# Two output projections as seven products of half blocks, with sums of weight blocks formed in DRAM

## The chip, the cores and the metric

The kernel runs on one core of a Trainium2 chip. The metric is device time in microseconds (us) of one execution, and the median of several runs is quoted. The engines are TensorE (PE, matmuls; its weight loads are listed as PEld), VectorE (DVE), ScalarE (ACT), GpSimd (POOL) and SyncE (SP, which here only issues transfers). Work is handed from engine to engine by semaphores, and each engine runs its own list of instructions in order.

## What is computed

A trunk of two layers on 512 tokens of 1024 channels, in float32. Each layer is: RMS norm, one wide input projection, mixers with gates, one output projection from 2048 to 1024 channels, residual add. A last RMS norm follows. What matters here are the two output projections:

```python
def even_layer(x, norm_g, w_in, pool_w, pool_scale, ws, bs, w_out):
    h = rmsnorm(x, norm_g)
    z = h @ w_in
    ...
    return x + jnp.concatenate([y_a, y_b], axis=-1) @ w_out

def odd_layer(x, norm_g, w_in, conv_w, w_out):
    ...
    return x + jnp.concatenate([y_c, y_d], axis=-1) @ w_out

def reference(...):
    ...
    return rmsnorm(h, final_norm)
```

## The kernel before, in words

Tokens are cut into four tiles of 128, channels into tiles of 128. Every operand of a large product is split into a high part (rounded to the type float32r, a copy on ScalarE) and a low part (the rest, a subtraction on VectorE); a product is the sum of three matmuls: high by high, high by low, low by high (`mm3`, lines 87 to 90). Weights come in chunks of 1 MB (128 partitions x 2048 elements): `weights` (line 68) loads a chunk on SP's queue into one of three `raw` buffers (line 75), copies the high part on ScalarE (line 76) and subtracts the low part on VectorE (line 77), into two buffers each for high and low parts (`wh`, `wl`). The normalised input, transposed to channels by tokens, stands in `hth` and `htl` for the whole of a layer.

`project` (line 140) is the input projection of one chunk: two columns of 128 outputs, each 8 x 3 matmuls of 128x512, with the result in one PSUM bank, used by a function that is passed in. After each column `tick` may start a piece of deferred work (`after`). The even layer calls `project` 16 times, for a, ga, u and gb of four groups; a group ends with a product on GpSimd (line 293). The odd layer calls it for the gates of four pairs of heads and for three times eight heads, and then for dc, dx, db and gd of four channel groups. In between stands the attention: scores, softmax, merges of the three dilation groups, which GpSimd does with small copies (lines 432 to 450), transposes (line 461), and mixing, which ends with a product on GpSimd (line 489).

The branch outputs are `y[0]` to `y[7]`, each 2 channel tiles x 512 tokens. `out_proj` (line 152) multiplies them by the output weights: eight chunks of 256 rows, each with the split of one `y` (lines 83 and 84); for each chunk four token tiles x two column halves x 2 x 3 matmuls of 128x512, all eight PSUM banks collecting sums over the eight chunks. The first six chunks run chunk by chunk. The last two are ordered by token tile by the function passed in: in the even layer `into_odd` (line 304) puts the residual add and norm of a tile (`normed`, line 93) and the transposes of the tile before (`to_channels`, line 115) between the matmuls of the next tiles; in the odd layer `finish` (line 529) normalises and writes a tile (line 535). In the trace these matmuls are named eo and oo, the weight parts heow, leow, hoow, loow. The odd layer begins with the values of the first pair (`near`), whose matmuls are 256 columns wide and named v.

The order in which instructions stand on each engine's list comes from a scheduler at build time, by readiness and by the order in which they are written; so a step may stand earlier than it is written.

Of the kernel before, what the change touches and what calls it, by code (L numbers as in the profile page):

```python
# [9 lines left out]
F32 = mybir.dt.float32  # L10
FR = mybir.dt.float32r
# [4 lines left out]
P = 128  # L16
# [14 lines left out]
def trunk(ctx, tc, x, w_even, w_eout, pool_w, ws_t, bs, par, g_even, w_odd, w_oout, g_odd, g_fin, cst, out):  # L31
# [4 lines left out]
    wp = ctx.enter_context(tc.tile_pool(name="wp", bufs=2))  # L36
    sp = ctx.enter_context(tc.tile_pool(name="sp", bufs=2))
    ps = ctx.enter_context(tc.tile_pool(name="ps", bufs=8, space=bass.MemoryType.PSUM))

    def bank(name):  # L40
        return ps.tile([P, S], F32, tag="ps", name=name)
# [16 lines left out]
    def gain(src, name):  # L58
        t = sp.tile([P, D], F32, tag="gain", name=name, bufs=1)
        nc.sync.dma_start(t, src.partition_broadcast(P))  # L60
        return t

    eps = cp.tile([P, 64], F32, name="eps")[:, 0:2]
    V.memset(eps, EPS)
    A.activation(eps[:, 1:2], eps[:, 0:1], AF.Sqrt)


    def weights(src, name, pieces=1):
        raw = wp.tile([P, CH], F32, tag="raw", name="r" + name, bufs=3)
        hi = wp.tile([P, CH], FR, tag="wh", name="h" + name, bufs=2)  # L70
        lo = wp.tile([P, CH], FR, tag="wl", name="l" + name, bufs=2)
        n = CH // pieces
        for i in range(pieces):
            at = slice(i * n, (i + 1) * n)
            nc.sync.dma_start(raw[:, at], src[:, at])
# [17 lines left out]
    def normed(tt, g, name, acc=None, then=None):  # L93
        o = sp.tile([P, D], F32, tag="xn", name=name, bufs=2)
        st = sp.tile([P, 64], F32, tag="st", name="st" + name, bufs=4)
# [18 lines left out]

    def to_channels(tt, o):
        for half in range(2):
# [15 lines left out]
    def tick(n=1):  # L132
        for item in list(pending):
            item[0] -= n
            if item[0] <= 0:
                pending.remove(item)
                item[1]()


    def project(src, name, use):  # L140
# [11 lines left out]
    def out_proj(src, name, last):  # L152
        acc = [[bank(f"{name}{t}{h}") for h in range(2)] for t in range(TT)]
        parts = {}

        def load(c):
            wh, wl = weights(src[c], f"{name}w{c}")
            parts[c] = (wh.rearrange("p (k d) -> p k d", k=2), wl.rearrange("p (k d) -> p k d", k=2),
                        *split(y[c], wp, "y", f"{name}y{c}"))

        def step(c, t, halves=(0, 1)):
            wh, wl, yh, yl = parts[c]
            tok = slice(t * P, (t + 1) * P)
            for h in halves:
                cols = slice(h * S, (h + 1) * S)
                for k in range(2):
                    mm3(acc[t][h], yh[:, k, tok], yl[:, k, tok], wh[:, k, cols], wl[:, k, cols],
                        c == 0 and k == 0, c == 7 and k == 1)

        for c in range(6):  # L170
            load(c)
            for t in range(TT):
                step(c, t)
        load(6)
        load(7)
        last(step, acc)

# [6 lines left out]
    with ExitStack() as ec:  # L184
# [6 lines left out]
        def v_half(c):  # L191
# [17 lines left out]
            if c == 0:  # L209
                load(0, 4)  # L210
                to_channels(0, normed(0, ge, "xa0"))
                nc.sync.dma_start(xt[:, 1, :], x[P:2 * P, :])
# [11 lines left out]
                for t in range(2):  # L224
                    step(t, 0)
                    step(t, 1)
                    to_channels(t + 1, o)
                    o = normed(t + 2, ge, f"xa{t + 2}")
                step(2, 0)
                to_channels(3, o)  # L230
                step(3, 0)
# [49 lines left out]
        def mixer_b(g, vb):  # L281
            mf = y[4 + g]
            mt = mf.rearrange("p d (n t) -> p d n t", n=TT)
            for d in range(2):
                acc = bank(f"mb{g}{d}")
                c0 = (g % 2) * 256 + d * P
                for n in range(TT):
                    T.matmul(acc[:, n * P:(n + 1) * P], vb[:, n, c0:c0 + P], wt[:, g, :], start=True, stop=True)
                V.tensor_add(mt[:, d], acc.rearrange("p (n t) -> p n t", n=TT),
                             bsb[:, g, None, :].to_broadcast([P, TT, P]))  # L290
            project(w_even[6 + 4 * g], f"u{g}", lambda j, acc: V.tensor_mul(mf[:, j, :], acc, mf[:, j, :]))
            sg = gate(w_even[7 + 4 * g], f"gb{g}")
            G.tensor_mul(mf, mf, sg)

# [8 lines left out]

    def into_odd(step, acc):
        def norm(t):
            o[t] = normed(t, go, f"xb{t}", acc[t])

        for t in range(2):
            step(6, t)
            step(7, t)  # L310
            norm(t)
        step(6, 2)
        to_channels(0, o[0])
        step(6, 3)
        step(7, 2)
        norm(2)
        to_channels(1, o[1])
        step(7, 3)
        norm(3)

    out_proj(w_eout, "eo", into_odd)


    slopes = [2.0 ** (-8.0 * (n + 1) / (SLOTS * N_DIL)) for n in range(SLOTS * N_DIL)]
    with ExitStack() as oc:
# [3 lines left out]
        def values(p):  # L329
# [142 lines left out]
        def mixed(h, v0, v12):  # L472
# [7 lines left out]
            for r in range(4):  # L480
                blk = slice(r * P, (r + 1) * P)
                for g in (1, 2):
# [5 lines left out]
                         yo.rearrange("p (b j r) -> p b r j", b=4, j=32))  # L488
            G.tensor_mul(y[h // 2][:, hc, :], y[h // 2][:, hc, :], yo)

        for p in range(SLOTS // 2):
            v0, v12, near, far = values(p)
# [35 lines left out]

    def finish(step, acc):
        for t in range(TT):  # L530
            for h in range(2):
                step(6, t, (h,))
                step(7, t, (h,))
            normed(t, gf, f"xc{t}", acc[t],
                   lambda h, v: nc.sync.dma_start(out[t * P:(t + 1) * P, h * S:(h + 1) * S], v))

    out_proj(w_oout, "oo", finish)


# [21 lines left out]
def _layout(i):  # L561
# [21 lines left out]

    def rows(w):
        return np.ascontiguousarray(np.asarray(w)[0].reshape(8, 2, P, D).transpose(0, 2, 1, 3)).reshape(8, P, CH)

# [3 lines left out]
        "w_even": w_even,  # L590
        "w_eout": rows(i["even_w_out"]),
        "pool_w": np.asarray(i["even_pool_w"])[0].reshape(4, 2, P, 256).transpose(0, 2, 1, 3).reshape(4, P, 512),
# [4 lines left out]
        "w_odd": w_odd,  # L597
        "w_oout": rows(i["odd_w_out"]),
        "g_odd": np.asarray(i["odd_norm"])[0],
# [20 lines left out]
```

## Time and profile before

| | us |
|---|---|
| median of 3 runs (lowest to highest) | 1124.02 (1122.96 to 1125.13) |
| the profiled execution, whole | 1124.62 |
| its span, first to last instruction | 1122.9 |
| TensorE busy | 1105.0 |
| VectorE busy | 452.0 |
| ScalarE busy | 357.5 |
| GpSimd busy | 142.6 |

The span is the time between the first and the last instruction of the profiled execution; 1.7 us lie around it. Busy time of an engine is the time that its instructions cover. TensorE's matmuls overlap, so a matmul's listed duration is longer than the distance to the next one. Idle time in square brackets stands before an instruction, with what ended it.

### The profile page before, as it was taken

The page shows a single profiled execution, that of the slowest core. Times are in us where ns is not written, and L with a number is a line of the kernel's source. Part 1 is how long each engine was busy: PE and PEld are TensorE (multiplying, and loading weights), DVE is VectorE, ACT ScalarE, POOL GpSimd, SP SyncE. Part 2 cuts the span into 40 slices and gives each one's busy share as a digit, 9 for nine tenths or more (in the row PEclk, how much of TensorE's full clock was granted, in tenths as well). Part 3 has the DMA queues.
Part 4 walks back from the last instruction along what each step waited for, and adds up shares of the span by engine and source line. Part 5 has one row for each costly group of instructions (what it writes and reads, how often), then busy time and mean ns, then how long its engine had stood idle before and what let it go on. Part 6 is the DMA issues. An engine that isn't in the chain of part 4 may idle for free.

```text
span 1122.9 us, 12809 instructions
## 1 busy us (share of the span) xinstructions
PE 1105.0 (98%) x5288; PEld 945.4 (84%) x5288; DVE 452.0 (40%) x617; ACT 357.5 (32%) x532; POOL 142.6 (13%) x460
## 2 busy tenths in 40 slices
PE   6999999999999999999999999999999999999997
PEld 5888888888888988899889988899888888888885
DVE  6344315343256225433345225442445442432326
ACT  5323223222235224432424224332424222121323
POOL 0001000101000004320224004220124011011000
PEclk9999999999999999999999999999999999999999
DMA  9232232322323231222221221322221222323211
GB/s 331 88 118 85 75 112 85 109 79 75 113 75 111 96 113 45 106 75 75 100 90 62 89 93 57 105 84 76 81 108 44 107 90 99 113 76 113 76 38 75
DMA packets 18282, 104.98 MB, mean 93 GB/s; under 512 B 2096, under 2 KB 3248, under 8 KB 6704
## 3 DMA queue, kind: packets, MB, share of 16 engines
q1 hardware_dynamic: 18224, 104.17, 26.5%
q8 instruction: 41, 0.67, 0.2%
q14 instruction: 17, 0.14, 0.0%
HBM read 102.06 MB, written 2.10 MB: 93 GB/s over the span
## 4 chain that ended last, share of the span: by engine, by line
PE 98%; DMA 1%; ACT 0%; DVE 0%; SPq 0%; issue 0%; DVEq 0%
PE q L90 8%; PE q L88 8%; PE q L89 8%; PE v L88 6%; PE v L90 5%; PE v L89 5%; PE oo L88 3%; PE eo L90 3%; PE eo L88 3%; PE oo L90 3%; PE eo L89 3%; PE oo L89 3%; PE gc L88 1%; PE gc L89 1%; PE gc L90 1%; PE dx L90 1%
## 5 line engine op out<-in xcount | busy, mean ns | idle before, releaser
L88 PE MATMUL q<-hth,hq 128*128 128x512 f32 x384 | 150.5, 392 | 0.0
L90 PE MATMUL q<-hth,lq 128*128 128x512 f32 x384 | 149.6, 389 | 0.0
L89 PE MATMUL q<-htl,hq 128*128 128x512 f32 x384 | 149.5, 389 | 0.0
L88 PE MATMUL v<-hv,hth 128*128 128x512 f32 (+1 forms) x320 | 114.8, 359 | 0.9 <-ACT hth L123 0.9
L90 PE MATMUL v<-hv,htl 128*128 128x512 f32 (+1 forms) x320 | 112.8, 353 | 0.0
L89 PE MATMUL v<-lv,hth 128*128 128x512 f32 (+1 forms) x320 | 112.6, 352 | 0.0
L90 PEld LDWEIGHTS q<-hth,lq 128*128 128x128 f32 x384 | 72.1, 188 | 15.1
L89 PEld LDWEIGHTS q<-htl,hq 128*128 128x128 f32 x384 | 72.1, 188 | 14.6
L88 PEld LDWEIGHTS q<-hth,hq 128*128 128x128 f32 x384 | 72.2, 188 | 14.4
L88 PEld LDWEIGHTS v<-hv,hth 128*128 128x128 f32 x320 | 76.6, 239 | 4.7 <-ACT hth L123 2.1
L90 PEld LDWEIGHTS v<-hv,htl 128*128 128x128 f32 x320 | 76.5, 239 | 3.2 <-DVE htl L124 0.7
L89 PEld LDWEIGHTS v<-lv,hth 128*128 128x128 f32 x320 | 76.8, 240 | 2.7
L77 DVE TENSOR_TENSOR lq<-rq,hq 128x2048 fp32r<-128x2048 f32 x24 | 54.9, 2289 | 51.2 <-ACT hq L76 51.2
L76 ACT ACTIVATE hq<-rq 128x2048 fp32r<-128x2048 f32 x24 | 46.0, 1915 | 76.5 <-PE q L89 55.4
L77 DVE TENSOR_TENSOR lv<-rv,hv 128x2048 fp32r<-128x2048 f32 (+1 forms) x22 | 37.4, 1704 | 39.2 <-ACT hv L76 39.2
L90 PE MATMUL eo<-heow,leoy 128*128 128x512 f32 x128 | 49.9, 390 | 0.0
L89 PE MATMUL eo<-leow,heoy 128*128 128x512 f32 x128 | 49.8, 389 | 0.0
L88 PE MATMUL eo<-heow,heoy 128*128 128x512 f32 x128 | 49.8, 392 | 0.0
L89 PE MATMUL oo<-loow,hooy 128*128 128x512 f32 x128 | 49.7, 389 | 0.0
L90 PE MATMUL oo<-hoow,looy 128*128 128x512 f32 x128 | 49.7, 389 | 0.0
L88 PE MATMUL oo<-hoow,hooy 128*128 128x512 f32 x128 | 49.5, 390 | 0.0
L76 ACT ACTIVATE hv<-rv 128x2048 fp32r<-128x2048 f32 (+1 forms) x22 | 31.6, 1446 | 55.8 <-PE v L90 17.0
(218 smaller groups left out, 2167.7 us busy)
## 6 DMA issues: line engine op xcount, KB each, us to landing
rq<-in_w_odd SPq DMA_DIRECT2D x24, 1024.0 KB, 4.7
rv<-in_w_odd SPq DMA_DIRECT2D x12, 1024.0 KB, 4.7
reow<-in_w_eout SPq DMA_DIRECT2D x8, 1024.0 KB, 4.8
roow<-in_w_oout SPq DMA_DIRECT2D x8, 1024.0 KB, 4.7
ra<-in_w_even SPq DMA_DIRECT2D x4, 1024.0 KB, 4.7
rga<-in_w_even SPq DMA_DIRECT2D x4, 1024.0 KB, 5.5
ru<-in_w_even SPq DMA_DIRECT2D x4, 1024.0 KB, 4.8
rgb<-in_w_even SPq DMA_DIRECT2D x4, 1024.0 KB, 4.7
```

What stands on the lines that cost most here:

```text
L76: A.activation(hi[:, at], raw[:, at], AF.Copy)
L77: V.tensor_sub(lo[:, at], raw[:, at], hi[:, at].bitcast(F32))
L88: T.matmul(acc, ah, bh, start=first, stop=False)
L89: T.matmul(acc, ah, bl, start=False, stop=False)
L90: T.matmul(acc, al, bh, start=False, stop=last)
```

## The change

Both output projections are written as a multiplication of 2 x 2 half blocks with seven products instead of eight. The y matrix is cut by tokens (two halves of 256) and channels (two halves of 1024), the weights by rows (1024) and columns (512). With blocks a(i,h) of y and b1 to b4 of the weights, sums and differences of y-blocks are formed on VectorE, in place; each of the seven y-blocks is split once into high and low parts (`form`). A product is 2 chunks of weights x 2 token tiles x 4 channel tiles x 3 matmuls, in two PSUM banks. Three pairs of banks, X, Z and Y, are used; products 1, 7, 5, 2, 6, 4, 3 follow each other in this order, and between them results are added to or subtracted from the residual `xt`, on VectorE from PSUM, and on GpSimd for what passes through SBUF (`s1`, `v`).

Four of the seven weight operands (4 to 7) are sums of blocks. They are formed in DRAM: 1 MB copies from DRAM to DRAM are put on SP's queue, one behind the weight load of each of the first eight input projections of the layer, and 1 MB transfers that add to the copy are issued by GpSimd: in the even layer four behind the product of group 1 and two each behind those of groups 2 and 3, in the odd layer two behind the product of each of heads 1 to 4. The sum 6 takes the sum 7 as operand, and the sum 4 takes the sum 6.

Weight parts get a third buffer: every third chunk goes into a pool opened when the layer's other pools are closed. The first y-block is split, and its difference formed, ahead of the end of the layer: in the even layer behind the last u, in the odd layer before the third channel group. `hth` and `htl` become two of three buffers that the split y-blocks use as well. At the end of the even projection token tiles 2 and 3 are done first, so the odd layer's first values begin with them.

```diff
-    hth = cp.tile([P, KT, S], FR, name="hth")
-    htl = cp.tile([P, KT, S], FR, name="htl")
-    y = [cp.tile([P, 2, S], F32, name=f"y{c}") for c in range(8)]
+    yy = cp.tile([P, 2 * KT, S], F32, name="yy")
+    y = [yy[:, 2 * c:2 * c + 2, :] for c in range(8)]
+    def ring(name):
+        return cp.tile([P, KT * S], FR, tag="act", name=name, bufs=3)
...
     def project(src, name, use):
         wh, wl = weights(src, name)
+        for out_proj in background:
+            out_proj.copy(marks["load"])
...
+        def copy(self, load):
+            with tc.issue_after(load.ins):
+                for dst, src in self.copies[:1]:
+                    nc.sync.dma_start(dst, src)
+                del self.copies[:1]
+        def add(self, n, work):
+            with tc.issue_after(work.ins):
+                for dst, src in self.adds[:n]:
+                    G.dma_start(dst, src, accum_op=ALU.add, max_dma_last_dim=2048)
+                del self.adds[:n]
+        def form(self, view, n):
+            f = ring(f"{self.name}f{n}").rearrange("p (w k t) -> p w k t", w=2, k=KT)
+            A.activation(f[:, 0], view, AF.Copy)
+            V.tensor_sub(f[:, 1], view, f[:, 0].bitcast(F32))
+            return f
+        def parts(self, n, q):
+            raw = raw_tile(f"r{self.name}{n}{q}")
+            nc.sync.dma_start(raw, self.src[n][q])
+            pool, bufs = (self.pool, 1) if self.chunks % 3 == 2 else (wp, 2)
...
+        def product(self, z, first, f, w, q, t, last=False):
...
+            for k in range(4):
+                kk = 4 * q + k
+                T.matmul(acc, f[:, 0, kk, tok], wh[:, k, :], ...)
+                T.matmul(acc, f[:, 0, kk, tok], wl[:, k, :], ...)
+                T.matmul(acc, f[:, 1, kk, tok], wh[:, k, :], ...)
+        def prepare(self):
+            b = self.block
+            self.f1 = self.form(b[0, 0], 1)
+            V.tensor_sub(b[0, 0], b[0, 0], b[0, 1])
...
+            both("X", True, self.f1, w1)
+            f7 = self.form(b[0, 0], 7)
+            w7 = [self.parts(7, q) for q in range(2)]
+            V.tensor_sub(b[0, 1], b[0, 1], b[1, 1])
+            f5 = self.form(b[0, 1], 5)
...
+            both("Y", False, f6, w6)
+            w4 = [self.parts(4, q) for q in range(2)]
+            f3 = self.form(b[1, 0], 3)
+            v = sp.tile([P, 2, S], F32, tag="xn", name=f"{nm}v", bufs=3)
+            for t in range(2):
+                V.tensor_sub(v[:, t, :], acc["Y", t], s1[:, t, :])
+                G.tensor_add(x(2 + t, 1), x(2 + t, 1), v[:, t, :])
+                G.tensor_sub(x(2 + t, 0), x(2 + t, 0), v[:, t, :])
+            both("Z", False, f4, w4, True)
+            w3 = [self.parts(3, q) for q in range(2)]
+            for t in range(2):
+                V.tensor_add(x(2 + t, 0), acc["Z", t], x(2 + t, 0))
+                half1(t)
+            for t in range(2):
+                for q in range(2):
+                    self.product("Y", False, f3, w3, q, t, True)
+                V.tensor_add(x(t, 1), acc["Y", t], x(t, 1))
+                half0(t)
...
+            if g == 3:
+                even_out.prepare()
             sg = gate(w_even[7 + 4 * g], f"gb{g}")
-            G.tensor_mul(mf, mf, sg)
+            even_out.add((0, 4, 2, 2)[g], G.tensor_mul(mf, mf, sg))
...
+    def norm1(t):
+        o[2 + t] = normed(2 + t, go, f"xb{2 + t}")
+    def norm0(t):
+        if not odd:
+            odd.extend(activations("ho"))
+        to_channels(2 + t, o[2 + t], *odd)
+        o[t] = normed(t, go, f"xb{t}")
+    even_out.run(norm1, norm0)
...
-                for c in range(2):
+                for c in (1, 0):
...
-                        if p == 0 and c:
-                            to_channels(2 + i, o[2 + i])
+                        if p == 0 and not c:
+                            to_channels(i, o[i], hth, htl)
...
+            work = G.tensor_mul(y[h // 2][:, hc, :], y[h // 2][:, hc, :], yo)
+            if h:
+                odd_out.add(2, work)
...
+            if c == 2:
+                odd_out.prepare()
```

## Rows read from the trace of the kernel before

**Rows 1.** Page, part 1: busy time of each engine, share, instructions.

```profile
PE 1105.0 (98%) x5288; PEld 945.4 (84%) x5288; DVE 452.0 (40%) x617; ACT 357.5 (32%) x532; POOL 142.6 (13%) x460
```

**Rows 2.** Page, part 4: the chain that ended last, by engine.

```profile
PE 98%; DMA 1%; ACT 0%; DVE 0%; SPq 0%; issue 0%; DVEq 0%
```

**Rows 3.** Stretches: length, busy time (instructions) by engine, PE clock, DMA share, GB/s.

```profile
240.00:253.60 13.60, 13.60 (x61) 11.27 (x61) 4.30 (x4) 2.52 (x2) 0.00 (x0) 1.00 0.23 78
253.60:342.70 89.10, 89.10 (x401) 73.61 (x401) 36.46 (x40) 29.80 (x34) 4.99 (x4) 1.00 0.25 85
...
1028.10:1115.60 87.50, 87.50 (x386) 71.80 (x384) 34.40 (x41) 26.70 (x32) 2.91 (x1) 1.00 0.18 65
1115.60:1122.90 7.30, 0.01 (x1) 0.00 (x0) 2.96 (x8) 1.10 (x4) 0.00 (x0) 0.68 0.23 88
```

**Rows 4.** Stretches inside eo and oo; busy order PE, PEld, DVE, ACT, POOL.

```profile
260.00:318.00 58.00, 58.00 (x257) 48.06 (x256) 17.59 (x10) 14.33 (x10) 1.13 (x4) 1.00 0.29 106
1046.00:1092.00 46.00, 46.00 (x205) 38.10 (x204) 14.07 (x8) 11.47 (x8) 0.00 (x0) 1.00 0.18 66
```

**Rows 5.** Groups by shape, VectorE: busy us, mean ns, idle before.

```profile
L77 DVE TENSOR_TENSOR loow<-roow,hoow 128x2048 fp32r<-128x2048 f32 x8 | 18.3, 2292 | 13.1 <-ACT hoow L76 13.1
...
L110 DVE SCALAR_TENSOR_TENSOR xb<-xt,stxb,go 128x512 f32<-128x512 f32 x8 | 5.7, 750 | 0.1
...
L99 DVE TENSOR_TENSOR xt<-oo,xt 128x512 f32<-128x512 f32 x8 | 5.5, 689 | 4.5 <-PE oo L90 4.5
```

**Rows 6.** Groups by shape, ScalarE.

```profile
L76 ACT ACTIVATE hoow<-roow 128x2048 fp32r<-128x2048 f32 x8 | 15.2, 1906 | 13.6 <-PE db L89 9.0 <-PE gd L89 4.6
```

**Rows 7.** Timeline (start, us, instruction) at the start of oo, ScalarE and VectorE.

```profile
1028.15 1.92 ACT L76 ACTIVATE hoow<-roow 128x2048 fp32r<-128x2048 f32 x1 [4.62 <-PE gd L89]
...
1030.10 2.29 DVE L77 TENSOR_TENSOR loow<-roow,hoow 128x2048 fp32r<-128x2048 f32 x1 [8.58 <-ACT hoow L76]
```

**Rows 8.** Timeline, GpSimd, two like products: VectorE idle, VectorE busy.

```profile
1023.61 1.31 POOL L519 TENSOR_TENSOR y<-cv,dc 128x512 f32<-128x512 f32 x1 [33.60 <-ACT dc L518]
1030.62 2.91 POOL L519 TENSOR_TENSOR y<-cv,dc 128x512 f32<-128x512 f32 x1 [5.71 <-ACT dc L518]
```

**Rows 9.** DMA issues: queue, count, KB each, median us to landing.

```profile
roow<-in_w_oout SPq DMA_DIRECT2D x8, 1024.0 KB, 4.7
...
out<-xc SPq DMA_DIRECT2D x8, 256.0 KB, 2.0
```

**Rows 10.** Timeline: a chunk's load issued on SP, its split on ScalarE.

```profile
978.02 0.33 SPq L75 DMA_DIRECT2D rgd<-in_w_odd  x1
...
1006.39 1.92 ACT L76 ACTIVATE hgd<-rgd 128x2048 fp32r<-128x2048 f32 x1 [8.48 <-PE dx L89]
```

**Rows 11.** Timeline: GpSimd's last product of the even layer.

```profile
256.14 4.02 POOL L293 TENSOR_TENSOR y<-y,sggb 128x1024 f32<-128x1024 f32 x1 [44.08 <-ACT sggb L245]
```

**Rows 12.** Chain and timelines: transposes in eo, the odd layer's first split, first transposed tile.

```profile
339.29 0.87 PE tx L119 x8
...
336.65 1.92 ACT L76 ACTIVATE hv<-rv 128x2048 fp32r<-128x2048 f32 x1 [2.17 <-issue]
...
338.60 2.29 DVE L77 TENSOR_TENSOR lv<-rv,hv 128x2048 fp32r<-128x2048 f32 x1
...
349.83 0.39 PE L88 MATMUL v<-hv,hth 128*128 128x256 f32 x1 [0.30 <-ACT hth L123]
```

**Rows 13.** GpSimd's timeline behind head 2, and the chain's transposes of head 3.

```profile
588.52 1.29 POOL L489 TENSOR_TENSOR y<-y,yo 128x512 f32<-128x512 f32 x1 [18.38 <-DVE yo L487]
595.39 0.19 POOL L432 COPY mn<-nm 128x4 f32<-128x4 f32 x1 [5.58 <-DVE nm L420]
...
607.44 3.69 POOL L450 COPY ff<-mn 32x2 f32<-32x2 f32 x16
...
611.48 0.77 PE tp L461 x7
```

**Rows 14.** Timeline, VectorE: the last residual add.

```profile
1115.65 0.69 DVE L99 TENSOR_TENSOR xt<-oo,xt 128x512 f32<-128x512 f32 x1 [0.73 <-PE oo L90]
```

More of the change, by code (lines that the diff above doesn't have):

```diff
@@ L37, in trunk @@
     sp = ctx.enter_context(tc.tile_pool(name="sp", bufs=2))
+    dp = ctx.enter_context(tc.tile_pool(name="dp", bufs=1, space=bass.MemoryType.DRAM))
     ps = ctx.enter_context(tc.tile_pool(name="ps", bufs=8, space=bass.MemoryType.PSUM))
@@ L61, in gain, with activations @@
         return t
+    def ring(name):
+        return cp.tile([P, KT * S], FR, tag="act", name=name, bufs=3)
+    def activations(name):
+        return tuple(ring(f"{name}{i}").rearrange("p (k t) -> p k t", k=KT) for i in "hl")
+    hth, htl = activations("he")
     eps = cp.tile([P, 64], F32, name="eps")[:, 0:2]
@@ L65, in trunk, with raw_tile @@
     A.activation(eps[:, 1:2], eps[:, 0:1], AF.Sqrt)
+    def raw_tile(name):
+        return wp.tile([P, CH], F32, tag="raw", name=name, bufs=3)
+    marks = {}
     def weights(src, name, pieces=1):
-        raw = wp.tile([P, CH], F32, tag="raw", name="r" + name, bufs=3)
+        raw = raw_tile("r" + name)
         hi = wp.tile([P, CH], FR, tag="wh", name="h" + name, bufs=2)
@@ L74, in weights @@
             at = slice(i * n, (i + 1) * n)
-            nc.sync.dma_start(raw[:, at], src[:, at])
+            marks["load"] = nc.sync.dma_start(raw[:, at], src[:, at])
             A.activation(hi[:, at], raw[:, at], AF.Copy)
@@ L93, in normed @@
     def normed(tt, g, name, acc=None, then=None):
-        o = sp.tile([P, D], F32, tag="xn", name=name, bufs=2)
+        o = sp.tile([P, D], F32, tag="xn", name=name, bufs=3)
         st = sp.tile([P, 64], F32, tag="st", name="st" + name, bufs=4)
@@ L113, in normed, with to_channels @@
         return o
-    def to_channels(tt, o):
+    def to_channels(tt, o, hth, htl):
         for half in range(2):
@@ L226, in v_half @@
                     step(t, 1)
-                    to_channels(t + 1, o)
+                    to_channels(t + 1, o, hth, htl)
                     o = normed(t + 2, ge, f"xa{t + 2}")
                 step(2, 0)
-                to_channels(3, o)
+                to_channels(3, o, hth, htl)
                 step(3, 0)
@@ L302, in trunk @@
     o = {}
[L304 to L321, printed above, removed]
+    odd = []
+    def norm1(t):
[6 more added lines that the diff above has]
+    even_out.run(norm1, norm0)
+    hth, htl = odd
     slopes = [2.0 ** (-8.0 * (n + 1) / (SLOTS * N_DIL)) for n in range(SLOTS * N_DIL)]
@@ L488, in mixed @@
                          yo.rearrange("p (b j r) -> p b r j", b=4, j=32))
-            G.tensor_mul(y[h // 2][:, hc, :], y[h // 2][:, hc, :], yo)
+            work = G.tensor_mul(y[h // 2][:, hc, :], y[h // 2][:, hc, :], yo)
+            if h:
+                odd_out.add(2, work)
+        odd_out = OutProj(w_oout, "oo")
+        background[:] = [odd_out]
         for p in range(SLOTS // 2):
@@ L527, in trunk, with finish @@
     gf = gain(g_fin, "gf")
[L529 to L537, printed above, removed]
+    def finish(t):
+        normed(t, gf, f"xc{t}", then=lambda h, v: nc.sync.dma_start(out[t * P:(t + 1) * P, h * S:(h + 1) * S], v))
+    odd_out.run(lambda t: finish(2 + t), finish)
 def _constants():
@@ L582, in _layout, with blocks @@
     w_odd = np.concatenate(parts)
-    def rows(w):
-        return np.ascontiguousarray(np.asarray(w)[0].reshape(8, 2, P, D).transpose(0, 2, 1, 3)).reshape(8, P, CH)
+    def blocks(w):
+        return np.asarray(w)[0].reshape(2, 2, 4, P, 2, S).transpose(0, 4, 1, 3, 2, 5).reshape(4, 2, P, CH)
     par = np.concatenate([np.asarray(i["even_pool_scale"])[0].reshape(8, P), np.asarray(i["odd_conv_w"])[0].reshape(24, P)])
@@ L590, in _layout @@
         "w_even": w_even,
-        "w_eout": rows(i["even_w_out"]),
+        "w_eout": blocks(i["even_w_out"]),
         "pool_w": np.asarray(i["even_pool_w"])[0].reshape(4, 2, P, 256).transpose(0, 2, 1, 3).reshape(4, P, 512),
@@ L597, in _layout @@
         "w_odd": w_odd,
-        "w_oout": rows(i["odd_w_out"]),
+        "w_oout": blocks(i["odd_w_out"]),
         "g_odd": np.asarray(i["odd_norm"])[0],
```

86 lines of the change are left out of this document (64 added, 22 removed).

## The prediction, made before the result was known

> **What bounds the kernel now.** I read the engine table first, then the chain of work that ended last, then busy time by stage, and only then single engines around the two output projections. TensorE is busy 98% of the span and VectorE 40% [rows 1]; the chain is TensorE for 98% of its length [rows 2], so only fewer or faster matmuls shorten it. By stage, the even output projection (eo) fills 253.6 to 342.7 us and the odd one (oo) 1028.1 to 1115.6 us; in both TensorE is busy throughout and VectorE 36.5 and 34.4 us [rows 3]. Behind oo stands a tail of 7.3 us, in which the last tile is normalised and written.
>
> A matmul's own duration (some 390 ns) must not be used for the saving: neighbours overlap. What counts is the distance between starts. A clean piece of eo holds 256 weight loads, one for each matmul, in 58.00 us, which is 0.2266 us each; oo gives 46.00 / 204 = 0.2255 [rows 4]. I take 0.2266.
>
> **Removed.** Each projection has 384 matmuls of 128x512. Seven half-block products of 2 token tiles x 8 channel tiles x 3 (high by high, high by low, low by high) make 336. So 48 go in each, 96 in all: 96 x 0.2266 = 21.75 us, all on the path, provided that nothing else makes TensorE wait. A product lasts 48 x 0.2266 = 10.88 us, a projection 76.1. The rest asks what is late.
>
> **VectorE and ScalarE inside a projection.** A split of a 128x2048 tile costs 1.91 us on ScalarE [rows 6] and 2.29 on VectorE [rows 5]. Weight chunks rise from 8 to 14; the eight splits of y give way to seven of y-blocks, of 128x2048; four block sums are new, same shape, two inputs, so 2.29 each. On VectorE that is (14 + 7 + 4) x 2.29 = 57.3, twelve reads of PSUM at 0.69 = 8.3 [rows 5], and four norms at 2 x 0.75 [rows 5] plus some 0.8 of small steps = 9.3; 74.9 in all. Three of the big ones (chunk 0, the first y-block, its difference) fit under the last input projection (4.3 us of VectorE work in 13.6 us before [rows 3]), and the last norm lies behind the end: 74.9 - 6.9 - 2.3 = 65.7 in 76.1 us, 86%. ScalarE: 21 x 1.91 = 40 and, as an estimate, 10 for squares, roots and copies, 66%. No engine exceeds TensorE, but VectorE gets near, so due times matter.
>
> Chunk n (24 matmuls, 5.44 us) takes the slot of chunk n-3, which is free 10.9 us before chunk n is due; the split needs 4.2. Counting VectorE work by due time from the start of the first product, with 1.9 for ScalarE ahead of it: by 10.9 us three big operations, ready at 8.8; by 21.8 us seven, ready at 17.9; by 32.6 us four more and two reads, ready at 28.5; by 43.5 us three more and two reads, ready at 36.7. Slack is 2 to 7 us everywhere, so I charge nothing; without that cover each missing us counts once for each projection. The one narrow place is chunk 1: its slot comes free only with the last input projection. Before, exactly this split starts at 1028.15 and ends at 1030.10 + 2.29 = 1032.39, which is 4.2 us after the last input projection released its slot [rows 7]; due after 5.44. It fits by 1.2; I charge 0.25 for each projection for a ScalarE step that slips in ahead.
>
> Buffers shared anew (the activations in a ring of three, the PSUM banks, a third xn) are free one product or more before they are taken; the reversed order of token tiles adds no instruction.
>
> **GpSimd.** Six 128x512 operations for each projection are new, and four of them form a chain (product 6 to the two upper tiles). Such an operation takes 1.31 us alone and 2.91 where it meets a 2.29 us operation of VectorE [rows 8]. The chain has from 12 matmuls before product 6 ends to 12 before product 4 ends for its first half, 10.9 us, and the same again 2.7 us later for its second. At 2.91 the halves are done after 6.5 and 12.3 us with the reads; the second then has about 1.3 us left. Charged nothing.
>
> **DMA.** A 1 MB load lands in 4.7 us, a 256 KB store in 2.0 [rows 9]. The loads of a projection become 14 x 4.7 = 66 us one after the other, in 76, and three buffers overlap them. The trace has no DRAM-to-DRAM copy: between 4.7 us (the write runs with the read) and 4.7 + 4 x 2.0 = 12.7. I take the lower half, since all 16 engines serve both. The copy stands on SP's queue between two loads and waits for nothing. The next load has time: before, one is issued at 978.02 and used at 1006.39, 28 us later, against 4.7 to land [rows 10]. Even 12.7 is hidden. An accumulating transfer reads twice and writes once: 4.7 to 2 x 4.7 + 8.0 = 17.4 us. All have one or more projections of time except the last two of the even layer, which are issued behind GpSimd's last product, 6.6 us into eo [rows 11], and whose load is due at 5 x 10.88 - 4.2 - 4.7 = 45.5. At 17.4 each they are done at 41.4. Charged nothing; at more than 19 us each every us counts twice. Behind that load on SP only its twin and later chunks wait.
>
> **The issue of the adds on GpSimd.** In the odd layer two are issued behind the product of each of heads 1 to 4. Behind heads 2 and 4 GpSimd has 5.58 us until the next head's merges, and these have no slack: the last merge copy ends at 607.44 + 3.69 = 611.13 and TensorE's transposes stand at 611.48 [rows 13]. The nearest row for an issue is SP's, 0.33 us [rows 10]; a pair is free up to 5.58. It can't gain. Charged nothing.
>
> **From eo into the odd layer.** Before, the first weights of the odd layer are split at 336.65 to 340.9, while eo still runs, and TensorE goes on at once [rows 12]. After, they take chunk 12's slot, which product 3 frees only 12 matmuls (2.7 us) before its end. Eight transposes (0.87 [rows 12]) come between. So 4.2 - 2.7 - 0.9 = 0.6 us of waiting at best, and with VectorE's due steps in the way (two norm halves at 0.75, an add at 0.69 [rows 5], two copies of transposed tiles of about that size) up to 4.2. I take 1.5, since before both halves of that split went in between the norms with no wait between them [rows 12]. The two transposed tiles behind it wait as they did before (0.3 us idle [rows 12]). The tail behind oo is unchanged: again one tile's add, at 1115.65 before [rows 14], and its norm.
>
> **Sum.** 21.75 - 1.5 - 2 x 0.25 - 0.5 (hand-overs at 14 product borders) = 19.3. The profiled execution took 1124.62, of which 1122.9 is its span; it is 0.6 above the median of the runs, 1124.02. So 1105.3 for it and 1104.7 for the median: 1105.
>
> **Rivals.**
> - Border queue (1113). The split of the odd layer's first weights stands behind both last norms on ScalarE and VectorE. Then it starts some 6 us after product 3 and ends 4.2 later: some 10 us of waiting in place of 1.5. For: it is written behind them. Against: before, it was written behind all four norms and still ran among them [rows 12]. 0.14.
> - VectorE and GpSimd become the bound (1109). If GpSimd gets no turn between VectorE's operations, the chain of four waits out three or four of them: 4 x 2.29 + 4 x 1.31 = 14.4 us for 13.6, and o of the upper tiles comes late to product 3's transposes; with VectorE at 86% this may grow to about 2 us in each projection's stream and again before the transposes: 4 us. For: 2.91 beside 1.31 [rows 8]. Against: the slack above. 0.14. The Trainium skill, "GPSIMD Engine Reference", section "Specifications", says that the two engines share their SBUF interfaces and collide on VectorE operations with two SBUF inputs; by that rule this rival holds wherever VectorE runs such operations back to back, and the trace agrees for a single one.
> - Adds that block (1128, slower). If GpSimd can't issue the second add of a pair until the first has drained, the pair holds it for 17.4 us and the merges of the heads behind 2 and 4 come 17.4 - 5.6 = 11.8 us late, straight onto TensorE: 23.6 us lost. From 15.2 us for a pair on, the whole gain is gone. Against: SP's issues never wait for landing. 0.05.
> - The sums don't come in time, or copies and adds starve the weight loads: the matmuls go but their time comes back as waits, 1108 to 1122. Against: DMA engines are busy a quarter of the time [rows 3]. 0.05.
>
> **Numbers.** Forecast 0.62. The forecast's low end charges nothing: 1124.0 - 21.75 = 1102.3, and 1101.5 with the short waits before chunks of the old stage gone as well. The high end takes in the border queue, 1114. That leaves out under 0.1 by case and some error of size. A change of 0.2%, 2.2 us, is about what a measurement can tell. Faster 0.92 (the forecast, the first two rivals and most of the last), same 0.03, slower 0.05.
>
> **What would show it.** Right: 336 matmuls of eo and of oo, each stage near 76 us, matmul spacing still 0.227, and one wait of 1 to 2 us in front of the odd layer's first values. Wrong: idle time of TensorE in front of a product's first matmul, released by VectorE (low parts) or by a load; GpSimd operations of over 3 us in product 4; transposes of heads 3 and 5 late; a wait of 10 us at the border.

## The result, and the profile after

The changed kernel takes 1106.91 us (median; 1106.23 to 1107.22) against 1124.35 us for the kernel before (1122.96 to 1125.13): a ratio of 0.9849, 95% interval 0.9837 to 0.9861. The forecast was 1105.0, the range 1101.5 to 1114.0. The profiled execution of after has a span of 1105.5 us, that of before 1122.9: 17.4 us less. First the engine table and the chain that ended last, the lines that answer to [rows 1, 2].

```profile
PE 1084.9 (98%) x5192; PEld 928.7 (84%) x5192; DVE 517.8 (47%) x643; ACT 390.9 (35%) x546; POOL 180.6 (16%) x488
...
PE 93%; issue 2%; DVE 2%; ACT 1%; POOL 1%; DMA 1%; SPq 0%; DVEq 0%; POOLq 0%; ACTq 0%
```

TensorE has 5192 matmuls in place of 5288: the 96 are gone. It is still busy 98% of the span, but its share of the chain has fallen from 98 to 93%: in some place the chain now runs through VectorE, ScalarE and GpSimd. The waits of TensorE (engine, line, who released it: us in total, times, longest) name the place:

```profile
PE eoZ L227 <- DVE leo L214: 2.0, 1, 2.0
PE ooZ L227 <- DVE loo L214: 0.9, 1, 0.9
```

Z at that point is product 7, the second of the seven; line 227 multiplies by the low part of a weight chunk, which VectorE makes at line 214. One such wait stands in each projection, always at the same product. The stretches of the two projections and of the tail, as in [rows 3]:

```profile
253.62:334.67 81.05, 79.01 (x346) 64.92 (x344) 67.10 (x57) 46.56 (x43) 17.12 (x12) 0.98 0.63 208
1020.87:1098.20 77.33, 76.45 (x337) 62.80 (x335) 64.95 (x54) 43.55 (x40) 13.02 (x7) 1.00 0.42 150
1098.20:1105.50 7.30, 0.16 (x1) 0.00 (x0) 3.19 (x9) 1.02 (x3) 0.00 (x0) 0.70 0.38 144
```

The odd projection is close to the forecast 76.1 us, the even one is 4 us longer than the odd one, and the tail has its 7.3 us as before. The even stretch shows a mean granted clock of 0.98 where it was 1.00. From first matmul to first matmul: from the start of eo to the start of oo before took 774.53 us (253.65 to 1028.18), after 767.25 (253.62 to 1020.87), 7.28 less; from there to the end 94.72 and 84.63, 10.09 less. Together these are the 17.4.

What product 7 waits for is read from three engines around it. TensorE at the start of product 7 in eo (start, duration, instruction, idle before and releaser), then ScalarE, VectorE and GpSimd ahead of it:

```profile
264.50 0.39 PE L226 MATMUL eoZ<-heo,eof 128*128 128x512 f32 x1
266.93 0.50 PE L227 MATMUL eoZ<-leo,eof 128*128 128x512 f32 x1 [2.04 <-DVE leo L214]
...
269.00 0.63 PE L228 MATMUL eoZ<-heo,eof 128*128 128x512 f32 x1
269.43 0.63 PE L226 MATMUL eoZ<-heo,eof 128*128 128x512 f32 x1
...
271.83 0.39 PE L226 MATMUL eoZ<-heo,eof 128*128 128x512 f32 x1
```

```profile
260.18 3.72 ACT L213 ACTIVATE heo<-reo 128x2048 fp32r<-128x2048 f32 x2 [2.33 <-POOL yy L418]
...
255.59 2.29 DVE L214 TENSOR_TENSOR leo<-reo,heo 128x2048 fp32r<-128x2048 f32 x1 [3.80 <-ACT heo L213]
260.18 2.29 DVE L254 TENSOR_TENSOR yy<-yy 128x2048 f32<-128x2048 f32 x1 [2.29 <-POOL yy L418]
262.39 2.29 DVE L202 TENSOR_TENSOR eof<-yy,eof 128x2048 fp32r<-128x2048 f32 x1
264.59 5.59 DVE L214 TENSOR_TENSOR leo<-reo,heo 128x2048 fp32r<-128x2048 f32 x2
...
256.12 4.02 POOL L418 TENSOR_TENSOR yy<-yy,sggb 128x1024 f32<-128x1024 f32 x1 [42.05 <-ACT sggb L368]
```

Two things hang on GpSimd's last product of the layer (256.12 to 260.14, the row of before in [rows 11]). The third weight chunk, the first of product 7, goes into the new pool, whose memory is free only when that product has read its operands: ScalarE's split of it starts at 260.18. And VectorE's next instruction is the difference of line 254, which reads the product's result; it waits 2.29 us for it, and behind it stand the low part of product 7's y block (line 202), which has nothing to do with that product, and the chunk's low part (line 214), which hangs on it only through the memory. So product 7, due at 264.7, gets its chunk at 266.9. The six matmuls behind the wait of 2.04 us still follow each other at 0.23 us; then eight come at 0.43, and the granted clock (third number from the end) is at the lower of its two levels, 1.2 GHz:

```profile
268.20:271.60 3.40, 3.40 (x10) 2.63 (x9) 3.40 (x2) 2.06 (x2) 3.12 (x1) 0.50 1.11 256
```

Product 7 of eo lasts 14.84 us (264.50 to 279.34) in place of 10.88, that of oo 12.05 (1031.75 to 1043.80): 5.1 us lost in the two.

### The profile page after: what moved, and what is told of

The parts are those of the page before. It is cut to its first block, busy times and chain, and to the rows that moved or that the text cites. A ratio compares the mean times of both kernels' runs of the same rounds, so it can differ in the third digit from the quotient of the medians.

```text
span 1105.5 us, 12746 instructions
## 1 busy us (share of the span) xinstructions
PE 1084.9 (98%) x5192; PEld 928.7 (84%) x5192; DVE 517.8 (47%) x643; ACT 390.9 (35%) x546; POOL 180.6 (16%) x488
## 4 chain that ended last, share of the span: by engine, by line
PE 93%; issue 2%; DVE 2%; ACT 1%; POOL 1%; DMA 1%; SPq 0%; DVEq 0%; POOLq 0%; ACTq 0%
PE q L102 8%; PE q L103 8%; PE q L101 8%; PE v L101 6%; PE v L103 6%; PE v L102 6%; PE gc L103 1%; PE gc L102 1%; PE gc L101 1%; PE u L103 1%; PE dc L102 1%; PE gd L102 1%; PE dx L101 1%; PE dc L101 1%; PE db L102 1%
## 5 line engine op out<-in xcount | busy, mean ns | idle before, releaser
L101 PE MATMUL q<-hoh,hq 128*128 128x512 f32 x384 | 150.6, 392 | 0.0
L103 PE MATMUL q<-hoh,lq 128*128 128x512 f32 x384 | 149.6, 390 | 0.0
L102 PE MATMUL q<-hol,hq 128*128 128x512 f32 x384 | 149.6, 390 | 0.0
L101 PE MATMUL v<-hv,hoh 128*128 128x256 f32 (+1 forms) x256 | 88.6, 346 | 0.3 <-ACT hoh L136 0.3
L102 PE MATMUL v<-lv,hoh 128*128 128x256 f32 (+1 forms) x256 | 87.2, 341 | 0.1
L103 PE MATMUL v<-hv,hol 128*128 128x256 f32 (+1 forms) x256 | 87.1, 340 | 0.0
L103 PEld LDWEIGHTS q<-hoh,lq 128*128 128x128 f32 x384 | 72.1, 188 | 15.1
L102 PEld LDWEIGHTS q<-hol,hq 128*128 128x128 f32 x384 | 72.1, 188 | 14.6
L101 PEld LDWEIGHTS q<-hoh,hq 128*128 128x128 f32 x384 | 72.2, 188 | 14.5
L102 PEld LDWEIGHTS v<-lv,hoh 128*128 128x128 f32 x256 | 64.4, 252 | 0.5 <-DVE lv L90 0.4
L418 POOL TENSOR_TENSOR yy<-yy,sggb 128x1024 f32<-128x1024 f32 x4 | 16.1, 4014 | 212.6 <-ACT sggb L368 212.6
L505 DVE COPY qk<-q 128x512 f32<-128x512 f32 x16 | 11.1, 692 | 76.9 <-PE q L103 76.9
```

Source lines behind the costliest of these rows:

```text
L101: T.matmul(acc, ah, bh, start=first, stop=False)
L102: T.matmul(acc, ah, bl, start=False, stop=False)
L103: T.matmul(acc, al, bh, start=False, stop=last)
L418: even_out.add((0, 4, 2, 2)[g], G.tensor_mul(mf, mf, sg))
L505: V.tensor_copy(t.rearrange("p (r j) -> p r j", r=4), acc.rearrange("p (j r) -> p r j", r=4))
```

## Experiments

Two theories stood against each other for the wait: VectorE's order (an operation that reads the result of GpSimd's product stands ahead of three that don't) and the third chunk's memory. A third question was what the copies and the adding transfers cost. Times are medians; the kernel before gave 1123.8 us beside them throughout.

### VectorE's order

```diff
-            V.tensor_sub(b[0, 1], b[0, 1], b[1, 1])
+            with tc.issue_after(self.low[7, 0].ins): V.tensor_sub(b[0, 1], b[0, 1], b[1, 1])
```

`self.low[7, 0]` is the operation that makes the low part of product 7's first chunk.

> Only VectorE's order is changed: the block difference b01 - b11 (line 254, which waits for GpSimd's last product at about 260.2 us in the even projection and 1026.3 us in the odd one) is put behind the low part of product 7's first chunk, so the three operations that product 7 waits for (its y block's low part, and its two weight chunks' low parts) no longer stand behind it. Theory A (VectorE's order makes the wait at product 7): product 7's y block is split at about 257.9 to 260.2, its second chunk's low part ends near 264.4 where it was 267.9; the wait of 2.0 us there goes, with it the eight matmuls at 0.43 us instead of 0.227 us (1.6 us), and the 0.9 us in the odd projection; 4.5 to 5 us less than the 1106.9 us of the changed kernel, about 1102.2. Rival B (the memory that the third chunk waits for is the whole cause): the same waits at line 227, 1106.9 +- 0.7. Rival C (the difference, now late, delays product 5's block): the wait moves to product 5 and the time stays at 1105 to 1107.

Measured: 1104.48 us (1103.55 to 1105.37), ratio 0.9828 (0.9815 to 0.9842), 2.4 us under the changed kernel where A said 4.7. The waits of TensorE, then VectorE:

```profile
PE eoY L228 <- DVE eof L202: 1.7, 1, 1.7
PE ooY L228 <- DVE oof L202: 0.6, 1, 0.6
```

```profile
257.71 4.41 DVE L202 TENSOR_TENSOR eof<-yy,eof 128x2048 fp32r<-128x2048 f32 x1
262.04 4.48 DVE L214 TENSOR_TENSOR leo<-reo,heo 128x2048 fp32r<-128x2048 f32 x2
266.45 3.38 DVE L254 TENSOR_TENSOR yy<-yy 128x2048 f32<-128x2048 f32 x1
269.75 3.39 DVE L262 TENSOR_TENSOR yy<-yy 128x2048 f32<-128x2048 f32 x1
```

Product 7 no longer waits: A's mechanism holds, and B falls. But the wait is now at product 5, one product later, as C had it. The reason stands in the durations. The operation that should have taken 2.29 us beside GpSimd's product took 4.41: it started at 257.71, GpSimd's product ended at 259.97, and it ended 2.15 us after that. The two block operations behind took 3.38 and 3.39 us beside GpSimd's subtractions of line 266. That is 4.3 us of stretching which no theory had counted. Behind the wait of 1.71 us the granted clock stays at 1.00:

```profile
277.60:286.00 8.40, 8.40 (x37) 6.97 (x38) 8.40 (x6) 5.65 (x3) 0.00 (x0) 1.00 0.64 244
```

### The third chunk's memory

```diff
-            sg = ep.tile([P, 2, S], F32, tag="sg", name="sg" + name, bufs=1)
+            sg = sp.tile([P, 2, S], F32, tag="sg", name="sg" + name, bufs=1)
```

> Only where a tile lives: the even layer's gate tile is moved to another pool, so that the pool of the third chunk opens over memory that no longer waits for GpSimd's last product; the odd layer is unchanged and serves as the control. VectorE still does the block difference that waits for GpSimd ahead of product 7's split. Theory A (order): chunk and block of product 7 are still behind that difference in VectorE's queue, but the chunk's split is done early, so that only one operation of 2.3 us stands behind it and ends at about 264.7 us, just when product 7 is due: the wait of 2.0 us in the even projection falls to 0.3 or less and the eight slow matmuls go, about 3.5 us, 1103.4; the odd projection's wait of 0.9 us stays. Rival B (memory): the even wait goes wholly, 1103.0. Rival C (neither): 1106.9 with the same wait.

Measured: 1103.20 us (1102.56 to 1103.60), ratio 0.9816 (0.9803 to 0.9830). VectorE in eo, then the wait that is left:

```profile
259.26 2.29 DVE L254 TENSOR_TENSOR yy<-yy 128x2048 f32<-128x2048 f32 x1 [2.29 <-POOL yy L418]
261.47 2.29 DVE L202 TENSOR_TENSOR eof<-yy,eof 128x2048 fp32r<-128x2048 f32 x1
263.67 2.28 DVE L214 TENSOR_TENSOR leo<-reo,heo 128x2048 fp32r<-128x2048 f32 x1
```

```profile
PE ooZ L227 <- DVE loo L214: 0.9, 1, 0.9
```

VectorE still waits 2.29 us for GpSimd and still does the difference first, yet eo has no wait: the third chunk had been split before that, so one operation less stands between the difference and product 7's first use of a low part. The odd projection, left as it was, keeps its 0.9. So neither order nor memory is the whole cause. Three operations of 2.2 us behind GpSimd's end are one too many; taking any one of them out of that row is enough for product 7.

### GpSimd's last product on VectorE

```diff
-            even_out.add((0, 4, 2, 2)[g], G.tensor_mul(mf, mf, sg))
+            even_out.add((0, 4, 2, 2)[g], (V if g == 3 else G).tensor_mul(mf, mf, sg))
...
-                G.tensor_mul(y[4 + c][:, j, :], cv[j][:, 0:S], dc[j][:, 0:S])
+                (V if c == 3 else G).tensor_mul(y[4 + c][:, j, :], cv[j][:, 0:S], dc[j][:, 0:S])
```

> The last elementwise product of each layer's output (one of four, 4.0 us on GpSimd in the even layer, 2.9 us in the odd one) is done on VectorE instead, so that nothing that product 7 needs waits for GpSimd. Theory (GpSimd's last product is what releases both the third chunk's memory and the block difference): both waits at product 7 go, about 4.5 us less, 1102.2. Rival (VectorE, which has little room in the first product of the projection, takes on 1 to 2 us more there and is late in its turn): wait of 1 to 3 us at product 1 or 7, 1105 to 1108.

Measured: 1101.34 us (1101.29 to 1102.19), ratio 0.9802 (0.9789 to 0.9815): the lowest median here, though level with the 1101.51 and 1101.61 of two runs below, and faster than both kernels. No wait at lines 226 to 228 is left. VectorE ahead of product 7:

```profile
257.07 1.22 DVE L418 TENSOR_TENSOR yy<-yy,sggb 128x1024 f32<-128x1024 f32 x1
258.20 2.29 DVE L202 TENSOR_TENSOR eof<-yy,eof 128x2048 fp32r<-128x2048 f32 x1
260.40 4.49 DVE L214 TENSOR_TENSOR leo<-reo,heo 128x2048 fp32r<-128x2048 f32 x2
264.81 3.39 DVE L254 TENSOR_TENSOR yy<-yy 128x2048 f32<-128x2048 f32 x1
```

The product costs VectorE 1.22 us in place of 4.02 on GpSimd, with nothing to wait for, and the split beside it takes 2.29 again and not 4.41. All seven products of eo now start 10.88 us apart (252.89, 263.77, 274.65 and so on; only the last holds transposes as well): 48 x 0.2266, to the hundredth. Against the changed kernel's profiled execution the gain is 5.90 us: 4.09 between the starts of eo and oo, 1.08 behind that, and 0.73 ahead of eo, where nothing was changed. (The first matmul of eo lies between 252.70 and 253.69 us in the kernels of this section, so up to 1 us between two executions is of that kind.) The edit moves one thing more: the layer's last two adds no longer stand behind a product on GpSimd, and it issues them at 219.67 and 225.62 us instead of at 260.09. That they are not what product 7 waited for is shown by the next runs, which have no adds.

### Without copies and adds

Operands 4 to 7 are loaded from plain blocks; `copies` and `adds` stay empty.

```diff
-            self.src = {1: b11, 2: b21, 3: b22, **sums}
+            self.src = {1: b11, 2: b21, 3: b22, 4: b21, 5: b11, 6: b11, 7: b12}
```

> The kernel leaves out the sums of weight blocks: no copies and no accumulating DMAs, products 4 to 7 load plain blocks instead; all else is the same work. It measures what the 16 copies and 16 accumulating DMAs cost. Theory (they lie beside TensorE's work; no load that they delay reaches the chain): 1106.9 +- 0.7, with the same wait at product 7. Rival (their traffic or GpSimd's time issuing them delays loads, splits or GpSimd's products): faster by over 1 us, with the wait of 2.0 us at product 7 smaller.

Measured: 1105.71 us (1104.92 to 1107.27), ratio 0.9838 (0.9825 to 0.9852), its range across that of the changed kernel. In the profiled execution the wait is the same, at the same place, and so is the clock behind it; the stretch from 264 to 275 us of the changed kernel, then of this one:

```profile
264.00:275.00 11.00, 8.96 (x32) 6.90 (x32) 11.00 (x5) 6.26 (x5) 5.06 (x2) 0.84 1.10 257
```

```profile
PE eoZ L222 <- DVE leo L209: 2.0, 1, 2.0
...
264.00:275.00 11.00, 8.96 (x33) 6.89 (x32) 11.00 (x5) 7.14 (x6) 5.05 (x2) 0.84 0.53 192
```

The DMA share falls from 1.10 to 0.53, the granted clock stays at 0.84: the slower matmuls don't come from transfers. The median is 1.2 us lower. This is probably the clock too: of the five executions the two with a listed mean clock of 0.996 span 1105.2 and 1105.6 us (one of them is the profiled one), the two with 0.998 span 1103.2; but only one of the five was traced. So the question was put again on a kernel without the wait (the product on VectorE, and no sums):

> The run with the last product of each layer's output on VectorE (1101.3 us), and in addition the sums of weight blocks left out: no copies, no accumulating DMAs, products 4 to 7 load plain blocks. Where the first run without sums stood on a kernel with two waits whose size may itself differ between executions, this one has none. Theory (copies and adds are hidden wholly): 1101.3 +- 0.4. Rival (they cost what the first run without sums seemed to give, 1.2 us): 1100.1.

Measured: 1101.61 us (1100.82 to 1101.96), ratio 0.9802 (0.9789 to 0.9815), against 1101.34 with the sums. Copies and adds cost nothing that can be measured.

### One product twice

```diff
             both("X", True, self.f1, w1)
+            both("X", True, self.f1, w1)
```

> The changed kernel with product 1 made twice (eight products; the second pass starts the sum anew, so the output is the same): 96 more matmuls, and 10.9 us more until product 7 is due. Theory A (TensorE sets the time at 0.2266 us a matmul, and the waits at product 7 come only from its three VectorE operations being 2.0 and 0.9 us late): 96 x 0.2266 = 21.75 us more, and the two waits with their slow matmuls (2.2 + 1.6 + 1.0 = 4.8 us) go: 1106.9 + 21.75 - 4.8 = 1123.9, with no wait above 0.3 us at line 227. Rival B (the lost 4.8 us belong to something that a later due time doesn't cure, such as the pool or the transfers): 1128.7.

Measured: 1123.44 us (1122.71 to 1123.91), ratio 0.9997 (0.9988 to 1.0005). A is met within 0.5 us. With 10.9 us more until product 7 is due, no wait at line 227 is left, and in eo the doubled product lasts 21.76 us (253.56 to 275.32). So the waits were a matter of the due time, and a product of 48 matmuls is worth its 10.88 us. It also says that the change with eight products would have brought nothing and cost nothing (1123.8 before): with that much room the sums, the extra splits and the extra buffers are free, and only the missing product pays.

### GpSimd beside VectorE

On top of the changed order of the first experiment:

```diff
-                G.tensor_sub(x(t, 1), x(t, 1), s1[:, t, :])
+                V.tensor_sub(x(t, 1), x(t, 1), s1[:, t, :])
```

> The run with the block difference behind product 7's operations, which left a wait of 1.7 us (even) and 0.6 us (odd) at product 5, and in addition the two subtractions of the product-1 result from x (line 266) on VectorE instead of GpSimd, behind the operations that product 5 waits for. Theory (GpSimd's two subtractions, 6.70 us, stretch VectorE's two block operations beside them from 2.28 to 3.38 and 3.39 us): these take 2.28 again, product 5's y block is ready 2.2 us earlier and the waits at product 5 go: 1104.5 - 2.3 = 1102.2. Rival (the 3.4 us are VectorE's own, from their operands): both still last 3.4 us and the waits stay, 1104.5, or 1105 with VectorE's extra 2 x 0.69 us.

Measured: 1101.51 us (1101.26 to 1102.04), ratio 0.9802 (0.9789 to 0.9816), 3.0 us under the run with the order alone; no wait at the products is left. The same two block operations:

```profile
266.22 2.28 DVE L254 TENSOR_TENSOR yy<-yy 128x2048 f32<-128x2048 f32 x1
268.42 2.28 DVE L262 TENSOR_TENSOR yy<-yy 128x2048 f32<-128x2048 f32 x1
```

Their 3.38 and 3.39 us were GpSimd's doing. Two subtractions more on VectorE (0.68 us each) and VectorE is in time; GpSimd's help had cost it 1.1 us for each operation beside it.

### A longer wait

```diff
-            V.tensor_sub(f[:, 1], view, f[:, 0].bitcast(F32))
+            for _ in range(3 if n == 7 else 1):
+                V.tensor_sub(f[:, 1], view, f[:, 0].bitcast(F32))
```

> The run with the last product on VectorE, which has no wait at product 7, and in addition the low part of product 7's y block made three times (same result), 2 x 2.2 us more on VectorE ahead of product 7's first chunk. That chunk's low part then ends near 267.0 us where 264.0 is due in the even projection and near 1029.6 for 1027.2 in the odd one: waits of 3.0 and 2.5 us by that alone, 1101.3 + 5.5 = 1106.8. Theory A (a wait of 2 us or more of TensorE brings the slower clock with it wherever it stands, as the 2.04 us wait did and the 0.88 us one did not): both waits are followed by some eight matmuls at 0.43 us in place of 0.227, 1.6 us each: 1110.0. Rival B (the slow matmuls belonged to the even stage's own load, its transfers or its GpSimd work): none behind the odd wait, 1106.8 to 1108.4.

Measured: 1119.87 us (1119.26 to 1122.19), ratio 0.9968 (0.9956 to 0.9979), far above 1110. The size was misjudged: the repeats don't stand in a row. VectorE does them in turn with the low parts of product 7's two chunks, so the last of them ends at 272.0; it and the operation ahead of it are stretched to 3.35 and 3.36 us. It is the y block, not the chunk, that is late:

```profile
PE eoZ L229 <- DVE eof L203: 6.7, 1, 6.7
PE ooZ L229 <- DVE oof L203: 6.1, 1, 6.1
```

```profile
272.02 0.80 PE L229 MATMUL eoZ<-heo,eof 128*128 128x512 f32 x1 [6.66 <-DVE eof L203]
272.61 0.63 PE L227 MATMUL eoZ<-heo,eof 128*128 128x512 f32 x1
...
1044.31 0.79 PE L229 MATMUL ooZ<-hoo,oof 128*128 128x512 f32 x1 [6.09 <-DVE oof L203]
1044.90 0.63 PE L227 MATMUL ooZ<-hoo,oof 128*128 128x512 f32 x1
...
1038.00:1049.00 11.00, 4.91 (x12) 3.72 (x12) 11.00 (x5) 4.26 (x3) 4.11 (x2) 0.71 0.43 158
```

The question itself is answered: the slow matmuls follow the wait in the odd projection too, so B falls, and A holds for waits of over 6 us. A wait of 2 us with slow matmuls behind it was seen in the even projection only. Product 7 lasts 20.60 us in eo (264.29 to 284.89) and 19.63 in oo (1037.16 to 1056.79), 18.5 us over 2 x 10.88, and 18.5 is what the run is slower than the run without the repeats. Of the 9.72 us in eo 6.82 are the wait and 2.9 the clock, of the 8.75 in oo 6.24 and 2.5. In the first run of this section, by contrast, a wait of 1.71 us was followed by matmuls at 0.23 us.

## Why the prediction was right, and where it was not

**Removed matmuls.** Right: 96 matmuls at the distance between starts. Products are 10.88 us apart wherever nothing waits, and one product added costs what one removed gains.

**Hand-overs between products, 0.5.** Nothing: the starts lie 10.88 us apart without a remainder. The old stage had small losses of its own, which the low end of the range had counted in: 384 x 0.2266 is 87.0 us, while eo before, without its two groups of transposes, took 87.5.

**VectorE's load.** The load was right, the due times were not. It is busy 67.1 and 65.0 us in the two projections, against 65.7. The step that failed is that chunk n's slot "is free 10.9 us before chunk n is due". For the third chunk there is no such predecessor; its slot is memory of the old layer, and GpSimd's last product still uses it. The count "by 10.9 us three big operations, ready at 8.8" then left out a fourth operation, the difference. The diff writes it behind product 7's chunks, but on VectorE's list it stands ahead of the y block's and the chunk's low parts, which only the trace after showed. That it reads the result of a product that GpSimd ends 6.6 us into eo could be seen before, from the diff and [rows 11]. From there 2.2 us each for the difference, the block's low part and the chunk's end at 13.2, where 11.1 was due. The prediction had used this very row of GpSimd for the adds, and not for this. In oo GpSimd's product ends 5.4 us into the projection, and the wait is 0.9.

**The narrow place.** It was put at chunk 1, with 0.25 us for each projection; chunk 1 was in time. The loss at product 7 was 4.0 us in eo (2.2 of waiting, the rest the slower clock, for which the sum had no term) and 1.2 in oo. By the prediction's own signs this counts against it: idle time in front of a product, released by VectorE's low parts, was the first sign of being wrong, and the one wait that it expected, in front of the odd layer's first values, did not come.

**The border, 1.5.** Too dear. The odd layer's first weights, its near values and the transposes around them, ScalarE, VectorE and TensorE:

```profile
332.19 1.92 ACT L89 ACTIVATE hv<-rv 128x2048 fp32r<-128x2048 f32 x1 [0.19 <-PE eoY L228]
...
334.14 2.29 DVE L90 TENSOR_TENSOR lv<-rv,hv 128x2048 fp32r<-128x2048 f32 x1
...
335.66 0.71 PE L132 MATMUL tx<-cs,xb 128*128 128x128 f32 x5
...
336.49 0.39 PE L102 MATMUL v<-lv,hoh 128*128 128x256 f32 x1
```

The weights' low part ends at 336.43, while the product ends at 334.67 plus some 0.2. I let eight transposes fill that time (0.9 us) and forgot the five that follow from the same tile (0.7 us), and the high part starts 0.2 us after product 3 frees its slot. What is left is about 0.2 us, within what the old border had. The rival "border queue" (1113) falls by the same rows: the high part at 332.19 stands between the two tiles' norms, as it did before.

**GpSimd.** Its chain of four on `v` lies where nothing disturbs it, four operations of 1.29 or 1.30 us from 311.66 to 316.7, so the 1.3 us of slack were several. Issuing adds is not SP's 0.33 us but 2.13 for a pair; it fits into the pause of 5.58 us [rows 13], of which 3.51 are left:

```profile
582.32 2.13 POOL L196 DMA_DIRECT2D oo<-in_w_oout  x2
587.96 0.19 POOL L555 COPY mn<-nm 128x4 f32<-128x4 f32 x1 [3.51 <-DVE nm L543]
```

Rival "adds that block" falls with this for pairs: GpSimd goes on 2.1 us after it begins to issue a pair, while the transfers land 8.2 to 8.5 us (the first) and 13.1 to 16.1 us (the second) after their issue in the odd layer. But what the rival feared is in the trace once, where four are issued in a row. GpSimd issues three from 142.20, stands for 5.24 us, and begins the fourth 0.25 us after the first has landed:

```profile
150.77 1.03 POOL L196 DMA_DIRECT2D eo<-in_w_eout  x1 [5.24 <-issue]
```

It did no harm there, because GpSimd's next product comes at 208.04. That it waited for that landing, and not for something else, is not shown.

**Copies and adds.** The estimates of 4.7 to 12.7 us for a copy and 4.7 to 17.4 for an add held for the medians (last column, us from issue to landing), not for every transfer: two of the four adds issued in a row took 19.5 and 20.0 us, the last of three copies issued within 3 us 16.0:

```profile
eo<-in_w_eout POOLq DMA_DIRECT2D x4, 1024.0 KB, 16.6
eo<-eo POOLq DMA_DIRECT2D x4, 1024.0 KB, 11.2
...
oo<-in_w_oout POOLq DMA_DIRECT2D x4, 1024.0 KB, 11.7
oo<-oo POOLq DMA_DIRECT2D x4, 1024.0 KB, 10.7
...
eo<-in_w_eout SPq DMA_DIRECT2D x8, 7.8
oo<-in_w_oout SPq DMA_DIRECT2D x8, 6.9
```

The 16.6 are of four issued in a row. That they cost nothing was right, and the runs without them show it. The rival "sums late or starved" falls too.

**VectorE and GpSimd become the bound, 1109.** Half right. The time it forecast is not the one that came, and its place (the chain of four) is wrong. But its cause, that the two engines stop each other, is part of what was lost. In oo GpSimd's last product takes 2.91 us beside VectorE, where a like one takes 1.31 [rows 8]; these 1.6 us are more than the wait of 0.9, though no run tests that alone. In the run with the order changed it was the whole remaining wait. The forecast knew only the one direction, GpSimd slowed beside VectorE [rows 8]; the runs show the other one as well.

**The sum.** 19.3 us were expected between the two profiled executions, 17.4 came: 21.8 less the 5.1 of product 7, and 0.7 more than nothing from the old stage's losses and the border. With the wait gone the time is 1101.3, just under the low end of the range, 1101.5, where that end had counted in the same two things. So the total came out near the forecast partly by luck, because two errors of opposite sign met: 2.0 us too much for border and hand-overs, and 4.6 too little at the second product of the projections.

## What to carry to other kernels

When work is taken from the engine that bounds, list for the first two due times of the shortened stage every operation that stands in the other engines' queues ahead of them, with the releaser of each, and not only those that are needed: an operation that waits for a slow engine makes all behind it late. A buffer in newly opened memory has a predecessor too: whoever last used that memory. And an elementwise product handed to GpSimd to relieve VectorE may cost VectorE more than doing it; here 1.2 us on VectorE replaced 4.0 on GpSimd and a wait.

## What the runs showed of the hardware

- VectorE and GpSimd hold each other up in both directions. VectorE's 128x2048 operation with two inputs takes 2.28 us alone and 3.36 to 3.39 beside GpSimd's 128x512 operations; behind a 4.02 us product that GpSimd had begun it took 4.41, ending 2.15 us after that product. GpSimd's 128x512 operation takes 1.3 us alone and, beside VectorE, 2.55 on the average of two in the changed kernel and 3.37 in the run with the order changed. 3.38 is about 2.28 and 1.1: they seem to go in turns, an operation of the one, then of the other. The Trainium skill, "SBUF — State Buffer", section "Who interferes with whom", says that a VectorE instruction with two inputs in SBUF contends with a GpSimd instruction that reads SBUF, and that the shared ports are locked rather than divided; the 4.41 and the 3.38 us agree.
- A single wait of TensorE in a stage that is otherwise full can lower the clock behind it. After 2.04 us six matmuls followed at 0.23 us and then eight at 0.43 (1.2 GHz); after 6.66 and 6.09 us the slow ones came at once, some twelve and ten; after 1.71 and 0.88 us all stayed at 0.23. So the wait of 2.0 us cost 4.0 in the profiled execution. It seems not to do so each time: of the four executions of the changed kernel three have a mean clock of 0.996 and span 1105.1 to 1105.5 us, the fourth 0.998 and 1104.4; only one was traced.
- A 1 MB transfer from DRAM to DRAM lands in 6.9 to 7.8 us (medians). One that adds lands in 8.2 to 8.6 us when nothing was issued just before it, and in 13.1 to 18.3 as the second of a pair (changed kernel); a pair occupies GpSimd for about 2.1 us while it is issued.
